# Two-layer hybrid decoder step on one core: gate's first low-rank product from mixed inputs, and three smaller moves

## Chip, core and metric

One core of one Trainium2 chip. The metric is device time of one execution in microseconds. The kernel before ran three times: 2744.53, 2752.41 and 2752.92 us, median 2752.41. A profiled execution took 2749.91 us. Engines: TensorE (PE, with its weight loads as PEld), VectorE (DVE), ScalarE (ACT), GpSimd (POOL) and SyncE (SP, which only issues transfers); ACT and POOL issue transfers too.

## Reference

One inference step of two layers for 1040 prompt tokens (16 of them meta tokens) and 8 decode tokens, width 1024, fp32. Layer 0 mixes tokens by a gated causal convolution of width 31, layer 1 by RWKV-7 with 16 heads of 64; each is followed by a squared-ReLU MLP of width 4096, and a last RMSNorm gives y. What the change touches:

```python
xx = prev - h                         # prev: the token before
xr, xw, xk, xv, xa, xg = (h + xx * x_mix[i] for i in range(6))
r, k, v = xr @ w_r, xk @ w_k, xv @ w_v
w_log = -softplus(-(w0 + tanh(xw @ w1) @ w2)) - 0.5
a = sigmoid((a0 + (xa @ a1) @ a2))
g = sigmoid(xg @ g1) @ g2             # g1: 1024 x 128
...
return out, full[:, -CONV_BUF:]       # conv state: the last 30 rows of every sequence
...
y = h * rsqrt(mean(h * h) + eps) * norm_final
```

The states (the last 30 convolution rows among them) are outputs beside y.

## The kernel before, in words

Values lie with the features on the partitions (8 tiles `k` of 128 features) and tokens along the free axis. Tokens go in groups: three for layer 0 and for the end of layer 1 (groups `g` of 352/348/348 and 328/352/352), four for the RWKV mixers (272/256/256/264, the last with the 8 decode tokens). The dense products of the MLPs and projections are split into a high and a low part and run as three matmuls each (L188 to L190: `hi*hi`, `hi*lo`, `lo*hi`). For these ACT casts a loaded weight (L158, `wo_hi`, `wi_hi`) and POOL subtracts the cast from it (L163, `wo_lo`, `wi_lo`); ACT squares and casts activations (L344, L141 `hh`), DVE makes their low part (L142 `hl`) and adds results to the residual (L355 `h`). A scheduler decides the order of the instructions on DVE, ACT, POOL and SP from priorities; on PE it is the order of the code in the long stages. Each engine works its own list strictly in order, and a transfer stands in the list of the engine that issues it.

**Layer 0, 250 to 600 us of the span.** PE runs the MLP of the first token group while DVE does the convolution of the next and PE and ACT do its decode tokens beside (`conv_dec`, L549). That loads the eight stored states in two tiles `sdec` of 120 rows x 1024, transposes them (L559, `pw`), copies them to `win` (L561), and per round `m` of 8 stores 29 rows x 1024 of them to the conv output (L564, `o_conv_sample`), on SP's list, with the MLP's weights around them.

**Preparation, up to 250 us.** Of the low-rank weights w1, a1 (64 columns each, side by side) and g1 (128 columns), ACT multiplies a copy with `x_mix` (L732), POOL subtracts it from the weights, and both, "own" and "prev", go to a scratch tensor `d_lr` in DRAM. With them `x_mix` needs no mixing of tokens: h times own plus the token before times prev.

**Mixers, 1080 to 1850 us.** For each group `prepare` (L858) gives hx (the group with one token ahead) and xx (DVE and POOL), and `mix(i, k)` (L877 to L880) makes one tile of mixed input on DVE, into a pool of 24 tiles: mix(0) for r, mix(2) for k, mix(3) for v, eight tiles each. `mixer_in` (L941) starts with `narrow_w` (L962) for the gate (`g_raw`, four tiles of 128x512) and the decays (`wa_raw`, four more from the same pool of four buffers), mix(0), `gate` (L991), the previous group's tail, then mix(3). `narrow` (L972) runs 16 matmuls on hx, shifted by one token for "prev" (L977, L978), and 8 more of 8 columns for the decode tokens in the last group (L980). ACT takes `p_g` by tanh into `lg` (L993, L994), `p_wa` into `lwa` (L988, L989). Behind it for every head pair `p`: keys, rates, values `pv`. Finished values go out to DRAM (`d_v`, L1041, L1045 on ACT); the chunks of 64 tokens read them back in `values(c)` (L1255), four transfers into `sv` and `uv` on ACT's list (L1262), and do the recurrence. Chunk 0 has its values once group 0 is done, in group 1's time.

**End, from 2260 us.** PE runs the MLP of groups 1 and 2 of layer 1; `final(g)` (L1574) makes the last norm. Group 0 sums squares over the eight feature tiles with `mean_parts` (L217): ACT squares, POOL and DVE add into one accumulator each (L231 `acc_f`), so PE only adds 2 tiles a block of 128 tokens (`fs`, L1597). Groups 1 and 2 keep eight squares (`fq`, L1585) and leave the sum to PE: 3 blocks x 8 tiles. Then the root (L1602, `os`), transposes (L1613, `pf`), scaling on DVE and ACT (L1616, L1618, `ot`, a half each) and two stores per block of half the width (L1620, L1622).

Of the kernel before, what the change touches and what calls it, by code (L numbers as in the profile page):

```python
# [16 lines left out]
P = 128  # L17
# [31 lines left out]
def hybrid_step(tc, x_prompt, x_sample, state_conv, state_shift, state_wkv, meta_tokens,  # L49
# [10 lines left out]
    with ctx:  # L60
# [25 lines left out]
        d_dec = dram.tile([6, DEC, D], F32, name="d_dec")  # L86
        d_lr = dram.tile([2, P, KT, 2, P], F32, name="d_lr")

# [29 lines left out]
        def vec(name, i):  # L118
            c = col[name] + i
            return pvec[:, c:c + 1]  # L120
# [269 lines left out]
        with ExitStack() as l0:  # L390
# [158 lines left out]
            def conv_dec(c, c_col):  # L549
# [5 lines left out]
                for m in range(KT):  # L555
# [7 lines left out]
                    nc.vector.tensor_mul(win, win, wdw[:, m:m + 1, :].broadcast_to([P, DEC, CW]))  # L563
                    nc.sync.dma_start(o_conv_sample[0, m, 0:CB - 1, :], sd[m // 4][m % 4 * CB + 1:(m % 4 + 1) * CB])  # L564
                    rd = decp.tile([P, DEC], F32, name=f"rd{m}", tag="rd")
# [119 lines left out]
            with ExitStack() as s:  # L685
# [38 lines left out]

                for i, parts in enumerate((((1, rwkv_w1[0]), (4, rwkv_a1[0])), ((5, rwkv_g1[0]),))):
                    own, prev = (xin.tile([P, D], F32, name=f"lr{i}{s_}", tag="xt").rearrange("p (k c) -> p k c", k=KT) for s_ in "op")
                    w = P // len(parts)
                    for q, (j, src) in enumerate(parts):
                        cs = slice(q * w, (q + 1) * w)
                        nc.sync.dma_start(own[:, :, cs], src.rearrange("(k p) c -> p k c", p=P))  # L730
                        for k in range(KT):
                            nc.scalar.activation(prev[:, k, cs], own[:, k, cs], AF.Copy, scale=vec("x_mix", j * KT + k))  # L732
                    for k in range(0, KT, 2):
                        nc.gpsimd.tensor_sub(own[:, k:k + 2], own[:, k:k + 2], prev[:, k:k + 2])
                    for s_, t in enumerate((own, prev)):
                        nc.sync.dma_start(d_lr[i, :, :, s_], t)
            hidp = pool(l0, "hidp0", 2)
# [203 lines left out]
        def mixer_in(g, tick):  # L941
# [19 lines left out]

            def narrow_w(i, name):  # L962

                out = []
                for q in range(HK):
                    raw = wide.tile([P, 4 * P], F32, name=nm(name, q) + "_raw", tag="wide")
                    v = raw.rearrange("p (a b) -> p a b", a=4)
                    nc.sync.dma_start(v, d_lr[i, :, 2 * q:2 * q + 2].rearrange("p k s c -> p (k s) c"))
                    out.append(v)
                return out  # L970

            def narrow(ws, name):  # L972
# [8 lines left out]
                return ps  # L981


            lg = lorap.tile([P, N1], F32, name=nm("lg"), tag="lg")
# [6 lines left out]
            def gate(ws):  # L991
                ps = narrow(ws, "g")
                nc.scalar.activation(lg[:, :n], ps, AF.Tanh, scale=0.5)  # L993
                nc.scalar.activation(lg[:, :n], lg[:, :n], AF.Copy, scale=0.5, bias=0.5)  # L994
# [260 lines left out]
        def values(c):  # L1255

            if c < NCH and c <= st["inv"] and c not in landed:
                landed.add(c)
                src = d_v[c * HS:(c + 1) * HS, :].rearrange("t (k q v) -> q t k v", q=2, v=HS)
                for t in (st["sv"], st["uv"]):  # L1260
                    for q in range(2):
                        nc.scalar.dma_start(t[HALF[1 - q], :, q, :], src[q])  # L1262

# [273 lines left out]
        with ExitStack() as l1:  # L1537
# [36 lines left out]
            def final(g):  # L1574
                lo, n = G2[g]
                hv = hl[g][:, :, :n]
                if g:
                    accs = [(actp, actp2)[g - 1].tile([P, cur["wide"]], F32R, name=f"fq{g}{k}", tag=f"acth{k}").bitcast(F32)
                            for k in range(KT)]
                else:  # L1580
                    accs = mean_parts(hv, n, f"f{g}", True, "facc")
                    yield 3
                for k in range(KT):
                    if g:
                        nc.scalar.activation(accs[k][:, :n], hv[:, k, :], AF.Square)  # L1585
                    if k % 2:
# [7 lines left out]
                for j, i in enumerate(starts):  # L1594
                    w = min(P, n - i)
                    for q, acc in enumerate(accs):
                        nc.tensor.matmul(ps[:w, j:j + 1], acc[:, i:i + w], ones_d[:, 0:1], start=q == 0, stop=q == len(accs) - 1)  # L1597
                ss = stat(f"os{g}", "os", 1, 4)
# [6 lines left out]
                for j, i in enumerate(starts):  # L1605
# [4 lines left out]
                    for hf in range(2):  # L1610
# [6 lines left out]
                        else:  # L1617
                            nc.vector.tensor_scalar(ot[:w, cs], pt[:w, :], ss[:w, j:j + 1], None, op0=ALU.mult)  # L1618
                        if np_:
                            nc.sync.dma_start(o_y_prompt[0, c:c + np_, cs], ot[:np_, cs])  # L1620
                        if np_ < w:
                            nc.sync.dma_start(o_y_sample.rearrange("b t d -> (b t) d")[:, cs], ot[np_:w, cs])  # L1622
                    yield 5
# [89 lines left out]
```

## Time and profile before

| | us |
|---|---|
| median of three runs | 2752.41 |
| profiled execution | 2749.91 |
| its span | 2748.2 |
| TensorE busy | 2641.3 |
| VectorE busy | 1716.6 |
| GpSimd busy | 1443.8 |
| ScalarE busy | 1122.1 |

The span is the time from the first to the last instruction of the profiled execution; 1.7 us lie around it. Its mean granted TensorE clock was 0.982 of full speed. A row of the timeline has start and duration in us, engine (a `q` behind it means its instruction queue, for issued transfers), line, operation, out<-in, and how many instructions the row stands for; a bracket gives the idle time ahead of it and what ended that. Matmul rows of fp32 stand for two instructions each. A row of busy time by stretch has the stretch and its length, busy time of PE, PEld, DVE, ACT and POOL with their instructions, granted clock, share of the 16 DMA engines and GB/s.

### The profile page before, as it was taken

How to read it: one execution, taken by the hardware profiler on the slowest of the kernel's cores; microseconds unless marked ns; L12 is line 12 of the kernel's file. 1: busy time of each engine (PE TensorE's matmuls, PEld its weight loads, DVE VectorE, ACT ScalarE, POOL GpSimd, SP SyncE). 2: the span in 40 equal slices, each digit the busy share in tenths (PEclk: the TensorE clock that was granted, in tenths of full speed). 3: DMA queues.
4: the chain of work that ended last, by engine and by line, in shares of the span. 5: the costliest groups of instructions: out<-in, count | busy, mean ns of one | idle time of the engine just before them, and what ended most of it. 6: DMA issues, size and time to landing. Idle time of an engine off the chain costs nothing. (4 is left out here: it accounts for less than half of the span.)

```text
span 2748.2 us, 51718 instructions
## 1 busy us (share of the span) xinstructions
PE 2641.3 (96%) x19948; PEld 2480.3 (90%) x19948; DVE 1716.6 (62%) x3546; ACT 1122.1 (41%) x2095; POOL 1443.8 (53%) x2054
## 2 busy tenths in 40 slices
PE   8999799999999999999999999979999999999998
PEld 8999699999999999877787787769999899999998
DVE  6999699997445345244757457576679753344433
ACT  5546345444444333333434444444543532222222
POOL 6678578878878776022111112365678663333330
PEclk9999899999999999999999999989999999999999
DMA  6663444554447442667777787786776642222211
GB/s 183 172 187 109 130 139 122 157 172 142 138 139 208 138 139 85 199 191 194 200 188 206 190 195 174 186 219 163 193 224 182 168 131 71 69 70 70 70 47 43
DMA packets 625548, 412.30 MB, mean 150 GB/s; under 512 B 121679, under 2 KB 567311, under 8 KB 625301
## 3 DMA queue, kind: packets, MB, share of 16 engines
q1 hardware_dynamic: 544643, 359.55, 46.7%
q10 hardware_dynamic: 72130, 23.61, 4.1%
q0 software_dynamic: 8528, 25.83, 2.9%
q8 instruction: 157, 2.57, 0.4%
q14 instruction: 90, 0.74, 0.1%
HBM read 344.81 MB, written 64.07 MB: 149 GB/s over the span
## 5 line engine op out<-in xcount | busy, mean ns | idle before, releaser
L163 POOL TENSOR_TENSOR wo_lo<-wo_raw,wo_hi 128x256 fp32r<-128x256 f32 x736 | 544.1, 772 | 318.7 <-ACT wo_hi L158 315.7
L163 POOL TENSOR_TENSOR wi_lo<-wi_raw,wi_hi 128x256 fp32r<-128x256 f32 x640 | 472.2, 770 | 264.8 <-ACT wi_hi L158 257.3
L188 PE MATMUL out<-hh,wo_hi 128*128 128x352 f32 (+2 forms) x1536 | 502.1, 327 | 20.3 <-DVE hl L142 13.3
L190 PE MATMUL ps_in<-m_l,wi_hi 128*128 128x352 f32 (+2 forms) x1536 | 494.2, 322 | 4.9 <-DVE m_l L286 4.8
L188 PE MATMUL ps_in<-m_h,wi_hi 128*128 128x352 f32 (+2 forms) x1536 | 495.4, 323 | 0.6 <-ACT m_h L285 0.6
L189 PE MATMUL out<-hh,wo_lo 128*128 128x352 f32 (+2 forms) x1536 | 495.6, 323 | 0.0
L190 PE MATMUL out<-hl,wo_hi 128*128 128x352 f32 (+2 forms) x1536 | 494.6, 323 | 0.0
L189 PE MATMUL ps_in<-m_h,wi_lo 128*128 128x352 f32 (+2 forms) x1536 | 491.9, 320 | 0.0
L355 DVE TENSOR_TENSOR h<-h,out 128x352 f32<-128x352 f32 (+2 forms) x768 | 385.7, 511 | 163.9 <-PE out L190 161.8
L536 DVE SCALAR_TENSOR_TENSOR cv<-u,wdw,cv 128x348 f32<-128x348 f32 (+2 forms) x720 | 377.9, 574 | 0.7
L158 ACT CAST wo_hi<-wo_raw 128x1024 fp32r<-128x1024 f32 x184 | 192.8, 1048 | 342.8 <-PE out L190 165.8
L158 ACT CAST wi_hi<-wi_raw 128x1024 fp32r<-128x1024 f32 x160 | 167.7, 1048 | 396.4 <-PE out L190 197.5
L188 PEld LDWEIGHTS out<-hh,wo_hi 128*128 128x128 f32 x1536 | 292.5, 190 | 27.3 <-DVE hl L142 15.4
L190 PEld LDWEIGHTS ps_in<-m_l,wi_hi 128*128 128x128 f32 x1536 | 288.8, 188 | 9.1 <-DVE m_l L286 8.6
L189 PEld LDWEIGHTS out<-hh,wo_lo 128*128 128x128 f32 x1536 | 291.7, 190 | 0.8
L188 PEld LDWEIGHTS ps_in<-m_h,wi_hi 128*128 128x128 f32 x1536 | 289.8, 189 | 2.6 <-ACT m_h L285 1.1
L190 PEld LDWEIGHTS out<-hl,wo_hi 128*128 128x128 f32 x1536 | 290.8, 189 | 0.2 <-DVE hl L142 0.2
L189 PEld LDWEIGHTS ps_in<-m_h,wi_lo 128*128 128x128 f32 x1536 | 289.2, 188 | 0.7
L343 DVE SCALAR_TENSOR_TENSOR ps_in<-ps_in,rs_m 128x352 f32<-128x352 f32 (+2 forms) x192 | 100.5, 524 | 247.6 <-PE ps_in L190 247.2
L142 DVE TENSOR_TENSOR hl<-ps_in,hh 128x352 fp32r<-128x352 f32 (+2 forms) x192 | 98.7, 515 | 139.7 <-ACT hh L141 139.6
L906 PE MATMUL pv<-mx,wv_raw 128*128 128x256 f32 (+2 forms) x512 | 133.1, 406 | 6.7 <-ACT rk L1082 4.7
L344 ACT ACTIVATE ps_in<-ps_in 128x352 f32<-128x352 f32 (+2 forms) x192 | 85.1, 444 | 132.1 <-DVE ps_in L343 131.7
(363 smaller groups left out, 4701.5 us busy)
## 6 DMA issues: line engine op xcount, KB each, us to landing
wi_raw<-in_w_mlp_in_dram SPq DMA_DIRECT2D x160, 512.0 KB
wo_raw<-in_w_mlp_out_dram SPq DMA_DIRECT2D x160, 512.0 KB
wk_raw<-in_rwkv_w_k_dram SPq DMA_DIRECT2D x32, 512.0 KB
wr_raw<-in_rwkv_w_r_dram SPq DMA_DIRECT2D x32, 512.0 KB
wv_raw<-in_rwkv_w_v_dram SPq DMA_DIRECT2D x32, 512.0 KB
d_ab<-ab POOLq DMA_DIRECT2D x32, 512.0 KB, 4.9
pg_raw<-in_conv_w_pw_dram SPq DMA_DIRECT2D x24, 512.0 KB
pa_raw<-in_conv_w_pw_dram SPq DMA_DIRECT2D x24, 512.0 KB
```

The lines of the kernel that those rows point to most:

```text
L142: eng_lo.tensor_sub(lo, src, hi.bitcast(F32))
L158: nc.scalar.copy(hi[:, :a * b], raw[:, :a * b])
L163: eng_lo.tensor_sub(lo[:, cs], raw[:, cs], hi[:, cs].bitcast(F32))
L188: nc.tensor.matmul(ps, w[0], act[0], start=first, stop=False)
L189: nc.tensor.matmul(ps, w[1], act[0], start=False, stop=False)
L190: nc.tensor.matmul(ps, w[0], act[1], start=False, stop=last)
L343: nc.vector.scalar_tensor_tensor(s, s, 0.0, rs()[:, :n], op0=ALU.max, op1=ALU.mult)
L344: nc.scalar.activation(s, s, AF.Square)
L355: nc.vector.tensor_add(hv[:, 4 * i + m, :], hv[:, 4 * i + m, :], ps[:, :n])
L536: nc.vector.scalar_tensor_tensor(acc[m][:, :n], ug[:, m, j:j + n], wdw[:, m, j:j + 1], acc[m][:, :n], op0=ALU.mult, op1=ALU.add)
L906: nc.tensor.matmul(ps[:, :n], w[:, k, :], act[k], start=k == 0, stop=k == KT - 1)
```

## The change

1. The gate's product reads mixed inputs. `gate` runs 8 matmuls on mix(5, k), which DVE makes (8 tiles a group), with g1 as it is, loaded in two tiles of 128x4x128. It stands ahead of mix(0). The preparation of g1 (L732) goes.
2. `values(0)` goes from ACT's list to POOL's; the other chunks stay.
3. The eight stores of 29 rows (L564) go from SP's list to ACT's.
4. `final` of groups 1 and 2 uses `mean_parts` as group 0 does, and each block of y is stored with one transfer of full width (two where prompt and decode tokens share a block).

```diff
-                    nc.sync.dma_start(o_conv_sample[0, m, 0:CB - 1, :], sd[m // 4][m % 4 * CB + 1:(m % 4 + 1) * CB])
+                    nc.scalar.dma_start(o_conv_sample[0, m, 0:CB - 1, :], sd[m // 4][m % 4 * CB + 1:(m % 4 + 1) * CB])
...
-                for i, parts in enumerate((((1, rwkv_w1[0]), (4, rwkv_a1[0])), ((5, rwkv_g1[0]),))):
...
+                for cs, j, src in ((HALF[0], 1, rwkv_w1[0]), (HALF[1], 4, rwkv_a1[0])):
...
+            gate_w = lambda: narrow_w("g", [rwkv_g1[0].rearrange("(k p) c -> p k c", p=P)[:, q * HK:(q + 1) * HK] for q in range(2)])
+            rate_w = lambda: narrow_w("wa", [d_lr[:, 2 * q:2 * q + 2].rearrange("p k s c -> p (k s) c") for q in range(HK)])
...
             def gate(ws):
-                ps = narrow(ws, "g")
+                ps = bank(nm("p", "g"))[:, :n]
+                for k in range(KT):
+                    nc.tensor.matmul(ps, ws[k // HK][:, k % HK, :], mix(5, k), start=k == 0, stop=k == KT - 1)
...
-            wg, ww = narrow_w(1, "g"), narrow_w(0, "wa")
+            wg, ww = gate_w(), rate_w()
+            gate(wg)
             act = mixed(0)
-            gate(wg)
...
-                        nc.scalar.dma_start(t[HALF[1 - q], :, q, :], src[q])
+                        (nc.scalar if c else nc.gpsimd).dma_start(t[HALF[1 - q], :, q, :], src[q])
...
-                if g:
-                    accs = [(actp, actp2)[g - 1].tile([P, cur["wide"]], F32R, name=f"fq{g}{k}", tag=f"acth{k}").bitcast(F32)
-                            for k in range(KT)]
-                else:
-                    accs = mean_parts(hv, n, f"f{g}", True, "facc")
-                    yield 3
+                accs = mean_parts(hv, n, f"f{g}", True, "facc")
+                yield 3
...
-                        if np_:
-                            nc.sync.dma_start(o_y_prompt[0, c:c + np_, cs], ot[:np_, cs])
-                        if np_ < w:
-                            nc.sync.dma_start(o_y_sample.rearrange("b t d -> (b t) d")[:, cs], ot[np_:w, cs])
+                    if np_:
+                        nc.sync.dma_start(o_y_prompt[0, c:c + np_, :], ot[:np_, :])
+                    if np_ < w:
+                        nc.sync.dma_start(o_y_sample.rearrange("b t d -> (b t) d"), ot[np_:w, :])
```

Lines of the changed file stand 1 to 5 off in the rows below. PE in group 1, around the gate (`mx_5_k` are the new mixtures, `hx` the unmixed input, `vt` the next work), before and then after:

```order
L921 MATMUL pn_12755<-sq_6_13612,hsel 128x256
L977 MATMUL p_g<-hx_12728,g_0_raw 128x256
L978 MATMUL p_g<-hx_12728,g_0_raw 128x256
...
L977 MATMUL p_g<-hx_12728,g_3_raw 128x256
L978 MATMUL p_g<-hx_12728,g_3_raw 128x256
L1038 MATMUL vt_7_13690<-ident,vv_7_13530 128x128 x2
```

```order
L918 MATMUL pn_12742<-sq_6_13599,hsel 128x256
L993 MATMUL p_g<-mx_5_0_13636,g_0_raw 128x256
L993 MATMUL p_g<-mx_5_1_13639,g_0_raw 128x256
...
L993 MATMUL p_g<-mx_5_7_13657,g_1_raw 128x256
L1039 MATMUL vt_7_13681<-ident,vv_7_13517 128x128 x2
```

The gate keeps its place on PE with 8 matmuls where 16 stood.

ACT in group 1, from the gate's tanh to the decays' (`r` is the key norm's root that DVE's reciprocal waits for), before and then after:

```order
L994 ACTIVATE lg_13635<-lg_13635 128x256
L1041 DMA d_v<-vt_7_13691 128x2x128
L1045 DMA d_v<-vm_7_13697 16x128
L1262 DMA sv<-d_v 64x8x64
L936 ACT_TABLE_LOAD
L936 ACTIVATE r_13765<-r_13765 128x256
```

```order
L995 ACTIVATE lg_13622<-lg_13622 128x256
L1042 DMA d_v<-vt_7_13682 128x2x128
L1046 DMA d_v<-vm_7_13688 16x128
L933 ACT_TABLE_LOAD
L933 ACTIVATE r_13756<-r_13756 128x256
L1083 COPY rk_0_13782<-pr_0_13743 128x256
```

The reads of d_v no longer stand between its writes and the root. They stand on POOL behind `d_bv` of the last head pair and ahead of a memset of `ni` and of xx for group 2.

ACT in layer 0, around the stores of the conv rows, before and then after:

```order
L158 CAST wi_0_6_hi<-wi_0_6_raw 128x1024
L158 CAST wi_0_7_hi<-wi_0_7_raw 128x1024
L344 ACTIVATE ps_in_4_0_3297<-ps_in_4_0_3297 128x352
L141 CAST hh_4_3295<-ps_in_4_0_3297 128x352
L541 COPY u_124<-cv_3_3633 128x348
L158 CAST wo_0_2_0_hi<-wo_0_2_0_raw 128x1024
```

```order
L158 CAST wi_0_6_hi<-wi_0_6_raw 128x1024
L564 DMA out_dram<-sdec_3809 29x1024 x4
L158 CAST wi_0_7_hi<-wi_0_7_raw 128x1024
L564 DMA out_dram<-sdec_3810 29x1024
L344 ACTIVATE ps_in_4_0_3280<-ps_in_4_0_3280 128x352
L564 DMA out_dram<-sdec_3810 29x1024
L141 CAST hh_4_3278<-ps_in_4_0_3280 128x352
L564 DMA out_dram<-sdec_3810 29x1024 x2
L541 COPY u_124<-cv_3_3616 128x348
L158 CAST wo_0_2_0_hi<-wo_0_2_0_raw 128x1024
```

The eight stores stand between ACT's casts, the last two right ahead of the copy of cv and the cast of `wo_0_2_0`. On SP they stood around the load of `wi_0_9`, four ahead of it and four between it and `wo_0_3_0`; there these loads now follow each other.

More of the change, by code (lines that the diff above doesn't have):

```diff
@@ L86, in hybrid_step @@
         d_dec = dram.tile([6, DEC, D], F32, name="d_dec")
-        d_lr = dram.tile([2, P, KT, 2, P], F32, name="d_lr")
+        d_lr = dram.tile([P, KT, 2, P], F32, name="d_lr")
         vecs = [
@@ L723, in hybrid_step @@
                 nc.scalar.dma_start(d_v[META:HS, KT * HS:], zt[:HS - META].rearrange("p k t -> p (k t)"))
-                for i, parts in enumerate((((1, rwkv_w1[0]), (4, rwkv_a1[0])), ((5, rwkv_g1[0]),))):
[L726 to L736, printed above, removed]
+                own, prev = (xin.tile([P, D], F32, name=f"lr{s_}", tag="xt").rearrange("p (k c) -> p k c", k=KT) for s_ in "op")
+                for cs, j, src in ((HALF[0], 1, rwkv_w1[0]), (HALF[1], 4, rwkv_a1[0])):
+                    nc.sync.dma_start(own[:, :, cs], src.rearrange("(k p) c -> p k c", p=P))
+                    for k in range(KT):
+                        nc.scalar.activation(prev[:, k, cs], own[:, k, cs], AF.Copy, scale=vec("x_mix", j * KT + k))
+                for k in range(0, KT, 2):
+                    nc.gpsimd.tensor_sub(own[:, k:k + 2], own[:, k:k + 2], prev[:, k:k + 2])
+                for s_, t in enumerate((own, prev)):
+                    nc.sync.dma_start(d_lr[:, :, s_], t)
             hidp = pool(l0, "hidp0", 2)
@@ L960, in mixer_in, with narrow_w @@
             HK = KT // 2
-            def narrow_w(i, name):
+            def narrow_w(name, srcs):
                 out = []
-                for q in range(HK):
+                for q, src in enumerate(srcs):
                     raw = wide.tile([P, 4 * P], F32, name=nm(name, q) + "_raw", tag="wide")
                     v = raw.rearrange("p (a b) -> p a b", a=4)
-                    nc.sync.dma_start(v, d_lr[i, :, 2 * q:2 * q + 2].rearrange("p k s c -> p (k s) c"))
+                    nc.sync.dma_start(v, src)
                     out.append(v)
@@ L1596, in final @@
                     for q, acc in enumerate(accs):
-                        nc.tensor.matmul(ps[:w, j:j + 1], acc[:, i:i + w], ones_d[:, 0:1], start=q == 0, stop=q == len(accs) - 1)
+                        nc.tensor.matmul(ps[:w, j:j + 1], acc[:, i:i + w], ones_d[:, 0:1], start=q == 0, stop=q == 1)
                 ss = stat(f"os{g}", "os", 1, 4)
```

3 lines of the change are left out of this document (1 added, 2 removed).

## The prediction

> **What bounds the kernel now.** I read the page's busy times first, then busy time by stage, and last the rows around each edited line. The span and the engines' shares, from the page:
>
> ```profile
> span 2748.2 us, 51718 instructions
> PE 2641.3 (96%) x19948; PEld 2480.3 (90%) x19948; DVE 1716.6 (62%) x3546; ACT 1122.1 (41%) x2095; POOL 1443.8 (53%) x2054
> ```
>
> TensorE is busy 96% of the span, so a PE instruction taken away is worth its time unless something else is late at that place, and the other gains are PE's waits. By stage (length, then busy time of PE, PEld, DVE, ACT, POOL, then granted clock):
>
> ```profile
> 250.00:600.00 350.00, 328.56 (x2023) 322.79 (x2023) 319.06 (x645) 158.91 (x253) 268.39 (x369) 0.97 0.46 137
> 1140.00:1300.00 160.00, 152.18 (x957) 122.26 (x955) 58.43 (x145) 55.12 (x154) 33.24 (x62) 1.00 0.66 188
> 1640.00:1850.00 210.00, 188.90 (x2399) 157.52 (x2398) 146.51 (x325) 90.99 (x225) 82.91 (x140) 0.93 0.79 194
> 2260.00:2700.00 440.00, 440.00 (x2747) 439.96 (x2746) 180.30 (x346) 107.86 (x170) 158.67 (x224) 1.00 0.22 64
> 2700.00:2748.20 48.20, 39.84 (x289) 39.16 (x287) 17.52 (x39) 17.83 (x38) 0.00 (x0) 0.89 0.17 61
> ```
>
> Three stages are touched. At 250–600 PE idles 21.4 us and DVE is nearly as full (319 of 350). The mixers (1080–1850) leave PE 5 to 21 us idle a window while DVE has room. From 2260 PE never waits, until the last 48 us.
>
> **Gate, removed matmuls.** The groups of the gate's matmuls and of VectorE's mixtures (ns least/median/most), then, from PE's timeline, each token group's first gate row and the row that follows its last (start, duration):
>
> ```profile
> L977 PE MATMUL p_g<-hx,g_raw x64: 377/382/469, 1143.6 to 1634.3; 128*128 128x256 f32 x32, 128*128 128x272 f32 x16, 128*128 128x264 f32 x16
> L880 DVE SCALAR_TENSOR_TENSOR mx<-xx,pvec,hx x96: 460/484/1281, 1086.7 to 1613.7; 128x256 f32<-128x256 f32 x48, 128x272 f32<-128x272 f32 x24, 128x264 f32<-128x264 f32 x24
> ...
> 1143.61 0.62 PE L977 MATMUL p_g<-hx,g_raw 128*128 128x272 f32 x2
> 1150.95 1.31 PE L906 MATMUL pr<-mx,wr_raw 128*128 128x272 f32 x5
> 1275.91 0.59 PE L977 MATMUL p_g<-hx,g_raw 128*128 128x256 f32 x2
> 1282.82 0.49 PE L1038 MATMUL vt<-ident,vv 128*128 128x128 f32 x3
> 1441.68 0.59 PE L977 MATMUL p_g<-hx,g_raw 128*128 128x256 f32 x2
> 1448.59 0.38 PE L1038 MATMUL vt<-ident,vv 128*128 128x128 f32 x2
> 1626.38 0.61 PE L977 MATMUL p_g<-hx,g_raw 128*128 128x264 f32 x2
> 1635.10 0.42 PE L1038 MATMUL vt<-ident,vv 128*128 128x128 f32 x2
> ```
>
> The gate takes 7.34, 6.91, 6.91 and 8.72 us. Half of the matmuls go, and in the last group the eight 8-column ones as well, where 8 of 0.44 us (3.5) stay: 3.67 + 3.45 + 3.45 + 5.2 = 15.8 us. Nothing is waited for at these places now.
>
> The price is 8 more mixtures a group: 32 at 0.484 us, 15.5 us of DVE. They go into slots that DVE had earlier, and chunk by chunk mix(0) takes mix(3)'s old place and mix(3) a new one, after the previous group's last key matmul; in group 1 that is near 1276, and pv, its reader, ran at 1302.7. DVE idles over 60% of 1140–1300 and 30% of 1640–1850, which covers it. If nothing covered it, 8 × 0.484 = 3.9 us would be lost in each group (15.5 in all); I take 3 us, one group's share nearly, for the first group and for places where DVE's in-order queue is then late for something smaller.
>
> **Values(0) off ScalarE, group 1.** ACT's queue, DVE behind it, and PE behind both (the bracket: idle before, and what ended it):
>
> ```profile
> 1294.84 0.60 ACTq L1262 DMA_DIRECT2D sv<-d_v  x1
> 1295.47 1.28 ACT L936 ACT_TABLE_LOAD   x1 [11.29 <-DMA d_v<-vm]
> 1297.21 1.75 DVE L937 RECIPROCAL r<-r 128x256 f32<-128x256 f32 x1 [10.64 <-ACT r L936]
> ...
> 1285.95 2.32 PE L906 MATMUL pr<-mx,wr_raw 128*128 128x256 f32 x10
> 1293.58 0.70 PE L977 MATMUL p_wa<-hx,wa_raw 128*128 128x256 f32 x2 [1.64 <-DMA wa_raw<-d_lr]
> 1301.14 0.79 PE L1096 MATMUL l_w<-lwa,wa 64*128 64x256 f32 x1 [3.41 <-ACT lwa L988]
> 1302.68 5.82 PE L906 MATMUL pv<-mx,wv_raw 128*128 128x256 f32 x16
> ```
>
> ACT stood until the writes of d_v had landed, because the read of d_v was next in its queue; lwa came late and PE waited 3.41 us. With the read on POOL, ACT goes on at 1288; what stays is p_wa's own tanh (about 0.5 us): 2.9 saved. The 1.64 us on wa_raw go too, since two of its four loads no longer wait for buffers 2 and 3 of the gate's weights. And pv's 16 instructions took 5.82 us where 10 of pr took 2.32 (0.216 apart, so 3.6 for 16): 2.2 us, the slow stretch after the wait. Together 6.8. What POOL now holds back is its next rows, a memset and xx of the next group. By their order they are needed some tens of us later, so I cost them at nothing; without that cover it would be the same wait, about 7 us, moved.
>
> On that slow pv the Trainium skill, TensorE: Matmul & The Clock Gate, Part 1, says an array that has idled runs at half rate until some microseconds of work have passed. The rows agree here (0.36 us apart against 0.216); by it, a wait that moves elsewhere would take its slow matmuls along.
>
> **Group 2.** ScalarE's order puts lg ahead of the norm's table loads. The waiting row:
>
> ```profile
> 1453.89 2.93 PE L906 MATMUL pr<-mx,wr_raw 128*128 128x256 f32 x6 [2.26 <-ACT lg L993]
> ```
>
> The bank's reader was late by 2.26 us, and 6 instructions at 0.216 need 1.46 with their tail, not 2.93: 3.7 us. Mixers: 15.8 + 6.8 + 3.7 − 3 = **23.3 us**, bounds 11 (all new mixtures paid) and 26.5.
>
> **Conv rows (SP to ScalarE).** A 4 us stretch (last two columns: share of the 16 DMA engines, GB/s), the page's group of POOL's subtractions (busy us, mean ns), then rows of SP's queue, PE and ACT by time:
>
> ```profile
> 298.00:302.00 4.00, 3.46 (x23) 3.17 (x22) 4.00 (x10) 1.88 (x4) 3.04 (x5) 1.00 0.07 27
> L163 POOL TENSOR_TENSOR wo_lo<-wo_raw,wo_hi 128x256 fp32r<-128x256 f32 x736 | 544.1, 772 | 318.7 <-ACT wo_hi L158 315.7
> ...
> 292.93 3.28 SPq L564 DMA_DIRECT2D out_dram<-sdec  x3
> 301.13 0.41 PE L188 MATMUL out<-hh,wo_hi 128*128 128x352 f32 x1
> 301.35 14.54 SPq L564 DMA_DIRECT2D out_dram<-sdec  x4
> 318.75 0.43 PE L188 MATMUL out<-hh,wo_hi 128*128 128x352 f32 x1 [2.61 <-DVE hl L142]
> 335.49 1.04 ACT L158 CAST wo_hi<-wo_raw 128x1024 fp32r<-128x1024 f32 x1 [17.35 <-DMA wo_raw<-in_w_mlp_out_dram]
> 337.88 0.66 PE L559 MATMUL pw<-ident,sdec 120*128 120x120 f32 x2 [14.85 <-ACT win L561]
> ```
>
> A share of 0.07 is one of 16 engines: each 29-row store (118.8 thousand bytes) takes 4.4 us on it at 27 GB/s, all eight 35 us, and the weights queued between and behind them wait with them. SP stands 14.54 us to issue the last four, the weights behind them land at 335.5, and PE loses 14.85 + 2.61 and two gaps of under 1 us, 18.9 in all. (PE's releaser is put down to win; the cast of wo_raw came just before, so it is the weights.)
>
> After, the weights are on SP ahead of or without the rows, and ScalarE is the one that stands. On SP the three rows from 292.93 on took 3.28 us, the last of them until 296.2, when some three quarters of the first were through; so about three and a quarter fit outstanding. The eighth then issues when 4.75 are done: 293 + 4.75 × 4.4 = 314, less if more fit, more for weights that now share the engine: 310 to 318. Behind the eighth in ScalarE's queue are the copy of cv and the cast of wo_0_2_0, which ran at 296.7. Copy and cast take 1.5 us, and PE needs about three of POOL's subtractions (0.77 us each) after them, so it can go on some 3.7 us after the eighth issue, t. PE then starts at t + 3.7 what it ran at 301.1: a stall of 12.6 (t = 310) to 20.6 (t = 318). Against the 18.9 that go this is a gain of 6 to a loss of 2; at t = 314 **2 us are gained**, which I take. Bounds: 18.9 gained if ScalarE is never held (nearest row: x3 in 3.28 us), and 17 lost if it is held to the end of all eight, near 333 (nearest row: x4 in 14.54 us).
>
> The Trainium skill, DMA: Bandwidth & Descriptors, section Issuing engines are not separate DMA queues, says that transfers run on the same 16 engines whoever starts them. By that the rows keep their 35 us on one engine after the move, as my term has it, and no more than the issue order is won. No run here has yet shown two queues sharing that one engine.
>
> **Tail.** The small products of the last norm, the longest run of them, the accumulating adds as group 0 has them, and the last store's issue:
>
> ```profile
> L1597 PE MATMUL fs<-ones_d,fq x96: 164/250/250, 2709.9 to 2739.4; 128*128 128x1 f32 x64, 128*96 128x1 f32 x32
> 2736.33 3.28 PE fs L1597 x34
> L231 DVE TENSOR_TENSOR acc_f<-acc_f,sq_f x3: 486/1035/1039, 2155.3 to 2158.9; 128x328 f32<-128x328 f32 x3
> 2744.83 0.32 SPq L1622 DMA_DIRECT2D out_dram<-ot  x1
> ```
>
> 34 instructions in 3.28 us are 0.0965 us each; 36 go in each of groups 1 and 2. In group 1 that is 36 × 0.0965 = 3.5 us on an engine that never waits there: 3.3 taken, since 12 must now follow the adds. In group 2 the last 3.28 become about 1.0, but three DVE adds (0.5 to 1.04 each) come after the last squares, and the eight transposes in between hide about half: 1.7 gained. Four wide stores for eight halves: the last issue at 2744.83 comes about 2 us sooner, of which the transfers, already under way, give 1. Also 0.5 of interleaved products. **6.5 us**, bounds 3 (adds all exposed) and 9.
>
> **Rest.** The preparation loses eight scalings, subtractions and three DMAs in a stage where PE is full: nothing, from −1 to +1.
>
> **Sum.** 23.3 + 2 + 6.5 = 31.8 us off the profiled execution's 2749.91 (span 2748.2 plus 1.7 around it): 2718.1. The runs' median is 2752.41, 2.5 higher; I forecast **2718.5**.
>
> **Rivals.**
> (a) *The rows disappear from PE's path.* ScalarE is held briefly and the weights, on their own queue, are early: 17 us better, **2701**. For it: the two queues separate weights from rows. Against: SP's 14.54 us; the number of rows that wait in a queue should be the same.
> (b) *ScalarE is held until nearly all rows are out* (t near 331): 331 + 3.7 − 301.1 = 33.6 us of stall, 14.7 worse than before: **2735**. For it: weights on the same engine; against: the fourth row was issued within 4 us.
> (c) *The gate's gain is eaten by DVE:* only 11 of 23 in the mixers: **2730**. For it: VectorE is the busiest after PE in 1640–1850; against: its share of 70%.
> (d) *Wait moved, not removed:* POOL's queue now holds xx and d_p, group 1 keeps its 6.8: **2725**.
> (e) *Slower than before:* the place is 250–600, where ScalarE feeds conv and MLP in order. If the one engine gives the weights' packets two thirds of its turns, a row takes 13.2 us and the eighth issues 4.75 × 13.2 = 63 us after 293: t = 356, a stall of 58.6, 39.7 worse than before, against 29.8 gained elsewhere: **2760**. From t = 346 on the kernel is slower than before. Against: once the weights lie ready their turns end, and their buffers come free only as PE goes on.
>
> **How the numbers follow.** Forecast (conv within 6 gained and 4 lost, mixers 19–26) 0.56, its range 2712–2726; (a) 0.14; (b) 0.10; (c) 0.08; (d) 0.06; (e) 0.06. A measurement tells about 0.3% (8.3 us) from no change, so faster means below 2744: the forecast, (a) and (d), and (b) and (c) but for the case that both hold: 0.90; within 0.3% 0.06 (that case, and half of (e)); slower 0.04. The range goes from (a) with all bounds good, 2698, to (b) with (c), 2745.
>
> **What would show it.** p_g of each group is 3.5 us long and l_w waits under 1 us; in group 1 the reciprocal runs near 1287; lg of group 2 ends no PE wait. ScalarE's rows show four long issues ending at 310–318, and PE one stall there with no wait for wo_raw at 335. The last fs run has about ten instructions, and the last store is issued some 3 us after the last norm's square root, where it was 5.2 (2739.63 to 2744.83). Wrong would be: PE waiting for mx, ScalarE released before 303 or after 325, the weights still late, or POOL's xx ending a wait.

## Result and profile after

The changed kernel takes **2723.31 us**, median of four runs (2719.99 to 2725.47), against 2752.24 us of four runs before: ratio 0.9901, 95% interval 0.9887 to 0.9915. Run again beside three experiments it had 2727.33 us, ratio 0.9920 (0.9907 to 0.9934). Forecast was 2718.5, in a range of 2698 to 2745.

The profiled execution of the changed kernel took 2719.99 us, the shortest of the four. Its page begins (busy time and share of each engine, instructions):

```profile
span 2718.1 us, 51431 instructions
PE 2613.6 (96%) x19796; PEld 2456.3 (90%) x19796; DVE 1736.2 (64%) x3584; ACT 1114.4 (41%) x2083; POOL 1447.8 (53%) x2060
```

TensorE lost 27.7 us of work and the span 30.1 us; PE's share stayed at 96%. So the time came off as PE work, and nearly as much PE idle time as before is left (104.5 us of the span, 106.9 before). Where it lies is best seen by cutting every profile at the same instructions. The marks are: start of the span, first `ps_o` matmul (a product of layer 0), the cast of `wi_0_6` on ScalarE, last `ps_o` (of L188), first `p_g` of the four groups, first and last `ps_oo` (a product of layer 1; last of L188), the last norm's root (`os`), end. A column `→x` is the length in us from the mark before it to x, taken from the starts of those rows in the kernel's own trace (e1 to e12 are the experiments below; "rows" are the conv stores):

| kernel | →ps_o | →wi_0_6 | →last ps_o | →p_g0 | →p_g1 | →p_g2 | →p_g3 | →ps_oo | →last ps_oo | →os | →end |
|---|---|---|---|---|---|---|---|---|---|---|---|
| before | 228.0 | 61.0 | 561.3 | 293.3 | 132.3 | 165.8 | 184.7 | 170.7 | 423.5 | 519.0 | 8.6 |
| after | 225.8 | 58.7 | 562.3 | 293.5 | 127.4 | 162.0 | 180.8 | 167.1 | 420.8 | 510.9 | 8.8 |
| e9 after again | 227.1 | 58.7 | 563.2 | 293.0 | 126.8 | 163.9 | 179.8 | 170.2 | 421.0 | 511.0 | 8.7 |
| e1 values(0) ACT | 226.9 | 58.7 | 562.8 | 294.3 | 128.7 | 165.7 | 181.3 | 167.6 | 420.5 | 511.0 | 9.0 |
| e10 the same | 228.5 | 58.7 | 562.5 | 292.9 | 128.8 | 166.3 | 182.0 | 170.5 | 421.5 | 510.9 | 9.0 |
| e2 rows SP | 228.8 | 58.7 | 563.3 | 292.9 | 127.3 | 162.8 | 180.4 | 168.2 | 425.9 | 511.2 | 8.8 |
| e11 the same | 228.0 | 58.8 | 562.0 | 292.9 | 127.0 | 164.2 | 181.3 | 169.1 | 420.8 | 510.8 | 8.7 |
| e3 gate old | 225.6 | 59.1 | 562.2 | 292.7 | 130.6 | 164.4 | 185.6 | 171.0 | 423.0 | 510.8 | 9.4 |
| e4 rows wide | 229.2 | 58.7 | 538.8 | 295.1 | 126.9 | 162.9 | 181.7 | 167.9 | 419.3 | 510.8 | 8.7 |
| e5 rows 28+1 | 226.2 | 58.7 | 542.0 | 292.8 | 127.1 | 163.6 | 182.7 | 168.6 | 422.2 | 511.1 | 8.7 |
| e6 before, rows wide | 228.4 | 59.0 | 538.8 | 295.0 | 131.9 | 166.1 | 185.2 | 169.9 | 419.0 | 519.8 | 9.4 |
| e7 wide, xx POOL | 228.4 | 58.7 | 539.2 | 293.2 | 127.0 | 163.7 | 181.8 | 169.9 | 424.8 | 511.0 | 8.7 |
| e8 wide, y halves | 228.5 | 58.7 | 538.8 | 292.6 | 126.9 | 165.7 | 181.4 | 170.9 | 420.2 | 511.0 | 9.1 |
| e12 wide, values(0) ACT | 228.5 | 58.7 | 539.1 | 292.7 | 127.1 | 167.6 | 182.3 | 168.8 | 424.2 | 510.8 | 9.0 |

Read columns, and distrust differences of a single pair: kernels whose instructions are the same in a stretch differ there by up to 4 us in →ps_o and in the mixers' stretches and 7 in →last ps_oo, by under 0.5 us in →wi_0_6 (but for before itself) and by under 1 in →os.

**The gate.** Its matmuls and VectorE's mixtures, by line, from the changed kernel's trace (ns least/median/most, first and last start):

```profile
L993 PE MATMUL p_g<-mx,g_raw x64: 379/382/393, 1140.3 to 1613.8; 128*128 128x256 f32 x32, 128*128 128x272 f32 x16, 128*128 128x264 f32 x16
...
L877 DVE SCALAR_TENSOR_TENSOR mx<-xx,pvec,hx x128: 460/485/1287, 1083.1 to 1612.2; 128x256 f32<-128x256 f32 x64, 128x272 f32<-128x272 f32 x32, 128x264 f32<-128x264 f32 x32
```

The PE work is what was forecast: 64 instructions for 144. A mixture still takes 0.485 us in the median.

**Group 1**, in order of time, from the timelines of PE, DVE, ACT, POOL and SP of the changed kernel:

```profile
1275.36 1.28 ACT L933 ACT_TABLE_LOAD   x1 [2.89 <-DMA xa<-d_ab]
1277.10 1.75 DVE L934 RECIPROCAL r<-r 128x256 f32<-128x256 f32 x1 [2.24 <-ACT r L933]
1281.23 1.40 POOL L1263 DMA_DIRECT2D sv<-d_v  x2 [6.75 <-issue]
1283.93 0.70 PE L1097 MATMUL l_w<-lwa,wa 64*128 64x256 f32 x2
1283.99 0.55 SPq L866 DMA_DIRECT2D hx<-d_hn  x1
1284.95 3.72 PE L903 MATMUL pv<-mx,wv_raw 128*128 128x256 f32 x16
1296.29 1.17 DVE L870 TENSOR_TENSOR xx<-hx 128x256 f32<-128x256 f32 x2 [2.93 <-DMA hx<-d_hn]
1299.95 0.46 DVE L1110 SCALAR_TENSOR_TENSOR rk<-st,negs,pb 128x256 f32<-128x256 f32 x1
1300.47 1.22 PE L1097 MATMUL l_a<-lwa,wa 64*128 64x256 f32 x2 [6.05 <-DVE rk L1110]
1301.62 4.05 PE L903 MATMUL pv<-mx,wv_raw 128*128 128x256 f32 x12
```

Up to pv everything came as forecast: ScalarE goes on at 1275, the reciprocal follows, no wait at l_w, pv at full speed (3.72 us for 16), 17.3 us after the gate's start where it was 26.8. Then 6.05 us are given back one head pair later. PE's l_a waits for a bank (an accumulator) that VectorE's `rk` (L1110) has to read; in VectorE's list that stands behind xx of group 2, and xx waits for hx, whose load was issued only when p_wa, the last reader of the old hx, had run, and took 12 us to land. In the kernel before, VectorE stood at the same load, but PE came later and had no wait at l_a there:

```profile
1309.14 0.42 DVE L873 TENSOR_TENSOR xx<-hx 128x256 f32<-128x256 f32 x1 [2.96 <-DMA hx<-d_hn]
```

**Groups 2 and 3**, timelines of PE and ACT:

```profile
1448.63 0.63 ACT L1487 ACTIVATE eq<-ey 128x512 f32<-128x512 f32 x1 [2.84 <-DVE ey L1486]
1450.09 0.30 ACT L1490 ACTIVATE ems<-ems,eps_t 128x8 f32<-128x8 f32 x1 [0.83 <-DVE ems L1489]
1450.41 1.28 ACT L987 ACT_TABLE_LOAD   x1
1451.70 0.38 ACT L987 ACTIVATE lwa<-p_wa 64x256 f32<-64x256 f32 x1
1452.13 0.79 PE L1097 MATMUL l_w<-lwa,wa 64*128 64x256 f32 x1 [4.76 <-ACT lwa L987]
1453.67 4.82 PE L903 MATMUL pv<-mx,wv_raw 128*128 128x256 f32 x12
...
1618.63 1.60 PE L903 MATMUL pr<-mx,wr_raw 128*128 128x264 f32 x6 [1.54 <-ACT lg L994]
1621.57 0.66 PE L1463 MATMUL yn<-ident,ey 128*128 128x128 f32 x4 [1.33 <-ACT gg L1288]
```

In group 2 the 2.26 us at lg are gone, and the same ScalarE chain (output norm of earlier tokens, second piece: ey, eq, ems, a table load) now stands ahead of lwa: 4.76 us, and the 12 matmuls of pv after it take 4.82 us, where 16 took 3.72 in group 1. In group 3, lg is late by 1.54 us where nothing was waited for before, and gg behind it.

**Conv rows**, the timelines of ACT and PE:

```profile
288.79 5.15 ACTq L564 DMA_DIRECT2D out_dram<-sdec  x4
294.13 9.25 ACTq L564 DMA_DIRECT2D out_dram<-sdec  x2
303.43 0.45 ACT L141 CAST hh<-ps_in 128x352 fp32r<-128x352 f32 x1 [7.97 <-issue]
303.45 10.88 ACTq L564 DMA_DIRECT2D out_dram<-sdec  x2
304.49 0.66 PE L188 MATMUL out<-hh,wo_hi 128*128 128x352 f32 x1 [9.59 <-DVE hl L142]
314.37 0.45 ACT L541 COPY u<-cv 128x348 f32<-128x348 f32 x1 [10.49 <-issue]
317.81 0.66 PE L188 MATMUL out<-hh,wo_hi 128*128 128x352 f32 x1 [10.79 <-DVE h L355]
```

And busy time in two 4 us stretches of it (length; PE, PEld, DVE, ACT, POOL with instructions; granted clock; DMA share; GB/s):

```profile
298.00:302.00 4.00, 0.00 (x0) 0.00 (x0) 0.00 (x0) 0.00 (x0) 0.00 (x0) 0.50 0.06 25
310.00:314.00 4.00, 0.00 (x0) 0.00 (x0) 0.00 (x0) 0.00 (x0) 0.00 (x0) 0.50 0.07 27
```

ScalarE was released at 314.3 and PE went on 3.5 us later. The hold comes in two pieces, because hh between the stores is held as well: 9.59 + 10.79 = 20.4 us. In the two stretches shown the DMA share is that of one engine of 16, at 25 to 27 GB/s, and all four compute engines stand.

**End**, the last norm's sums by line:

```profile
L1592 PE MATMUL fs<-ones_d,acc_f x36: 166/250/271, 2231.5 to 2709.1; 128*128 128x1 f32 x24, 128*96 128x1 f32 x8, 128*72 128x1 f32 x4
```

The same matmuls in the last group, the root and the stores, in the timelines of PE, ACT and SP:

```profile
2697.92 14.75 SPq L1615 DMA_DIRECT2D out_dram<-ot  x6
2708.12 1.17 PE L1592 MATMUL fs<-ones_d,acc_f 128*128 128x1 f32 x10
2709.32 0.41 ACT L1597 ACTIVATE os<-fs,eps_t 128x2 f32<-128x2 f32 x2 [1.20 <-PE fs L1592]
2712.72 1.05 SPq L1617 DMA_DIRECT2D out_dram<-ot  x1
```

From the root to the end it is 8.8 us, as before, though the last store is issued 3.4 us after the root and not 5.2.

### The profile page after: what moved, and what is told of

The parts are those of the page before. It is cut to its first block, busy times and chain, and to the rows that moved or that the text cites. A ratio compares the mean times of both kernels' runs of the same rounds, so it can differ in the third digit from the quotient of the medians.

```text
span 2718.1 us, 51431 instructions
## 1 busy us (share of the span) xinstructions
PE 2613.6 (96%) x19796; PEld 2456.3 (90%) x19796; DVE 1736.2 (64%) x3584; ACT 1114.4 (41%) x2083; POOL 1447.8 (53%) x2060
## 5 line engine op out<-in xcount | busy, mean ns | idle before, releaser
L188 PE MATMUL out<-hh,wo_hi 128*128 128x352 f32 (+2 forms) x1536 | 502.3, 327 | 36.4 <-DVE hl L142 18.8
L188 PE MATMUL ps_in<-m_h,wi_hi 128*128 128x352 f32 (+2 forms) x1536 | 495.3, 322 | 1.2 <-ACT m_h L285 1.2
L355 DVE TENSOR_TENSOR h<-h,out 128x352 f32<-128x352 f32 (+2 forms) x768 | 385.8, 511 | 166.6 <-PE out L190 164.4
L188 PEld LDWEIGHTS out<-hh,wo_hi 128*128 128x128 f32 x1536 | 292.8, 191 | 42.9 <-DVE hl L142 20.8
L158 ACT CAST wo_hi<-wo_raw 128x1024 fp32r<-128x1024 f32 x184 | 192.9, 1048 | 328.2 <-PE out L190 166.5
L188 PEld LDWEIGHTS ps_in<-m_h,wi_hi 128*128 128x128 f32 x1536 | 290.1, 189 | 3.1 <-ACT m_h L285 1.8
L142 DVE TENSOR_TENSOR hl<-ps_in,hh 128x352 fp32r<-128x352 f32 (+2 forms) x192 | 98.6, 515 | 132.2 <-ACT hh L141 132.1
```

The lines of the kernel that those rows point to most:

```text
L142: eng_lo.tensor_sub(lo, src, hi.bitcast(F32))
L158: nc.scalar.copy(hi[:, :a * b], raw[:, :a * b])
L188: nc.tensor.matmul(ps, w[0], act[0], start=first, stop=False)
L355: nc.vector.tensor_add(hv[:, 4 * i + m, :], hv[:, 4 * i + m, :], ps[:, :n])
```

## Experiments

Runs e1 to e4, e5 to e8 and e9 to e12 each stand beside runs of the kernel before on the same chip; a ratio is to those. Of the theories set against each other, A says for the mixers that a wait that goes is followed by the next one, and for the conv rows that their shape, not the queue, is the cost.

**e1 and e10: values(0) back on ScalarE.**

```diff
-                        (nc.scalar if c else nc.gpsimd).dma_start(t[HALF[1 - q], :, q, :], src[q])
+                        nc.scalar.dma_start(t[HALF[1 - q], :, q, :], src[q])
```

> The changed kernel (2723.3 us) with values(0) back on ScalarE's list. Theory A: in group 1 the next limit, right behind the wait that the move took away, is the load of hx for group 2 (landed at 1296.3, VectorE's xx and the rk of L1110 behind it, PE's l_a waited 6.05 us), so undoing the move costs little: the wait at l_w comes back (2 to 4 us), l_a's wait shrinks by about as much, p_g of group 2 stays within 2 us of 1429.7; 2721 to 2726. Rival B: the move earned what the prediction had for it, 5 to 7 us that l_a's wait does not eat; then 2728 to 2731.

Measured 2728.35 us (2726.54 to 2737.71), ratio 0.9929 (0.9915 to 0.9943). By the time, B. But the 2723.3 us that it is held against come from another group of runs, so both kernels were run side by side:

> The changed kernel itself, beside the next three on the same chip, since stages with the same instructions have differed by up to 4 us between the profiles so far. Both theories: ratio to before 0.989 to 0.991, and a length of the stretch from group 1's first p_g to group 2's anywhere between 162 and 166 us.

> values(0) back on ScalarE's list, beside the changed kernel. Theory A (the load of hx ends group 1's waits in either order, l_a starts 32.5 to 33.5 us after p_g): within 3 us of the changed kernel's median of this call. Rival B (the move is worth 5 us or more, as the first run of this kernel had it): 5 us or more above it.

e9 has 2727.33 us (ratio 0.9920, just above the 0.989 to 0.991 expected; group 1's stretch 163.9, as expected), e10 2732.02 (2723.97 to 2733.31), ratio 0.9931 (0.9919 to 0.9944): 4.7 us above, between the two theories. PE's waits in group 1 of e10:

```profile
1290.73 0.70 PE L1097 MATMUL l_w<-lwa,wa 64*128 64x256 f32 x2 [2.38 <-ACT lwa L987]
1304.32 1.22 PE L1097 MATMUL l_a<-lwa,wa 64*128 64x256 f32 x2 [4.11 <-DVE rk L1110]
1359.71 1.13 PE L1229 MATMUL A<-xa,bk 64*128 64x128 f32 x14 [1.56 <-DVE nr L1239]
```

The first two rows are as theory A has them: the wait at l_w is back with 2.38 us, and l_a's has shrunk from 6.59 (e9) to 4.11; l_a starts 32.9 us after the gate (1271.4) here and 34.1 in e9. The theory missed what comes after: 3 to 4 us are lost in the recurrence and the second pair behind it. The third row, the matmul of tile `A` that waits for nr, is part of that and not in e9; what makes up the rest is not shown.

**e12: the same on the wide-copy kernel.**

> The wide-copy kernel (2701.7) with values(0) back on ScalarE's list: the same question without the hold of the conv rows ahead of it. Theory A: ratio to before within 0.001 of the wide copy's 0.9832. Rival B: 0.985 or above.

2708.78 us, ratio 0.9851 (0.9836 to 0.9866), against 0.9832 without it: B by a hair, with the wide copy's ratio from another group of runs.

**e3: the gate as before** (16 matmuls on hx, g1 prepared, behind mix(0); the other three parts as changed).

```diff
-                ps = bank(nm("p", "g"))[:, :n]
-                for k in range(KT):
-                    nc.tensor.matmul(ps, ws[k // HK][:, k % HK, :], mix(5, k), start=k == 0, stop=k == KT - 1)
+                ps = narrow(ws, "g")
...
```

> The changed kernel with the gate, its weights and their preparation as before (16 matmuls on hx, g1 prepared). Theory A: a shorter gate shows fully as time on PE in each group but is partly eaten by the next wait, so the old gate costs 11 to 16 us in the mixers, plus 2 us in the preparation stage if the scalings of g1 held that up: 2735 to 2742, with p_g of each group 6.9 to 8.7 us long. Rival B: the mixers lose the full 15.8 us and the waits in group 1 and 2 do not come back elsewhere: 2742 or above. Rival C: the preparation costs nothing and its 2 us in the changed kernel were a chance of the start: then ScalarE's cast of wi_0_6 stands within 1 us of the changed kernel's 284.5, else near 287 to 289.

2738.58 us (2736.07 to 2744.50), ratio 0.9964 (0.9950 to 0.9977): A for the time. For the preparation it is C: the cast of wi_0_6 stands at 284.7, the preparation costs 59.1 − 58.7 = 0.4 us in →wi_0_6, and the 2 us at the start belong to no part, since →ps_o runs from 225.6 to 229.2 over all kernels.

e3, e1, e10 and e12 make a table of two parts in the mixers (first p_g to first ps_oo, means of the kernels' sums in us): neither 653.3 (before, e6); values(0) moved alone 651.6 (e3); gate alone 645.6 (e1, e10, e12); both 640.7 (the changed kernel, e2, e4, e5, e8, e9, e11). So what a part is worth depends on the other: values(0) is worth 1.7 us alone and 4.9 on top of the gate, the gate 7.7 alone and 10.9 on top of values(0). These are means of few profiles (e3 is a single one, the sums with both parts run from 637.3 to 644.9), so the steps hold to some 3 us. In group 1's stretch alone: 166.0, 164.4, 166.5, 163.6. There the two parts together bring 2.4 us, less than the 3.45 of the gate's matmuls, and the gate alone brings nothing.

**e2 and e11: the conv rows back on SP.**

```diff
-                    nc.scalar.dma_start(o_conv_sample[0, m, 0:CB - 1, :], ...)
+                    nc.sync.dma_start(o_conv_sample[0, m, 0:CB - 1, :], ...)
```

> The changed kernel with the eight 29-row stores back on SP's list. Theory A: the stores last 35 us on one DMA engine either way, ScalarE's hold (PE waits of 9.59 and 10.79 us) costs what SP's hold of the weights did (18.9 in all) or 1 to 2 us more: 2721 to 2724, with PE waiting for weights near 330 and not for hl and h. Rival B: the move earned 2 us or more, as the prediction took it: 2725 or above.

2729.15 us (2725.68 to 2730.72), ratio 0.9922 (0.9911 to 0.9934): B by the time, but the stretch that holds the rows is 563.3 us against 562.3, and most of the rest lies at the start and in →last ps_oo, where the instructions are the same. So it was run again beside the changed kernel:

> The eight stores back on SP's list, beside the changed kernel. Theory A (the hold only changes its place): within 3 us of the changed kernel's median of this call. Rival B (the move is worth 5 us or more, as the first run had it): 5 us or more above it.

2726.30 us (2721.72 to 2731.07) against 2727.33: A. The stretch is 562.0 us against 563.2. With the stores on SP the hold is there too, at SP's issues and in PE's wait for the weights behind them (e2):

```profile
301.69 14.54 SPq L564 DMA_DIRECT2D out_dram<-sdec  x4
337.75 0.66 PE L559 MATMUL pw<-ident,sdec 120*128 120x120 f32 x2 [15.73 <-ACT win L561]
```

**e5: each store cut into 28 rows and 1 row**, on ScalarE's list at the same places.

```diff
-                    nc.scalar.dma_start(o_conv_sample[0, m, 0:CB - 1, :], ...)
+                    for r0, r1 in ((0, CB - 2), (CB - 2, CB - 1)):
+                        nc.scalar.dma_start(o_conv_sample[0, m, r0:r1, :], sd[m // 4][m % 4 * CB + 1 + r0:m % 4 * CB + 1 + r1])
```

> The changed kernel with each 29-row store cut in two, 28 rows and 1 row, on ScalarE's list at the same places. Theory A: what held ScalarE was the shape, since 29 rows of a store all went to one DMA engine; 28 rows spread over 14, so the two PE waits of 9.59 and 10.79 us go as they did with the wide copy: ratio to before 0.982 to 0.985, cast of wi_0_6 to the last ps_o 538 to 543 us. Rival B: what held it is the number of stores, or a source on few partitions, however it is cut: 560 us or more in that stretch, ratio 0.990 or above. In between (545 to 558) if the 16 issues themselves (0.3 to 0.6 us each) delay the casts.

2704.57 us (2701.11 to 2706.18), ratio 0.9833 (0.9819 to 0.9847), stretch 542.0: A. The first issues on ScalarE, and PE's waits where it had stood 9.59 and 10.79 us:

```profile
289.23 1.48 ACTq L565 DMA_DIRECT2D out_dram<-sdec  x4
290.84 0.67 ACTq L565 DMA_DIRECT2D out_dram<-sdec  x2
...
295.94 0.43 PE L188 MATMUL out<-hh,wo_hi 128*128 128x352 f32 x1 [0.43 <-DVE hl L142]
299.19 0.43 PE L188 MATMUL out<-hh,wo_hi 128*128 128x352 f32 x1 [2.03 <-DVE h L355]
```

Twice as many transfers with the same bytes, and an issue costs some 0.37 us, where pairs of the 29-row stores took 9.25 and 10.88: the shape was the cost.

**e4: one copy of all eight rows' blocks from the stored state to the output**, in DRAM, with 16 as the slowest dimension.

```diff
-                    nc.scalar.dma_start(o_conv_sample[0, m, 0:CB - 1, :], ...)
...
+                rows = lambda t: t.rearrange("m w d -> m (w d)").rearrange("m (a x) -> a m x", a=16)
+                nc.scalar.dma_start(rows(o_conv_sample[0, :, 0:CB - 1, :]), rows(state_conv[0, :, 1:CB, :]))
```

> The changed kernel with the eight stores replaced by one copy of the same rows from the stored state to the output in DRAM, cut so that the slowest dimension is 16 (16 x 8 x 1856 elements), issued once by ScalarE. Theory A: the stores held one of 16 engines for 35 us because 29 rows do not divide, and the hold was PE's only reason to wait there: the waits of 9.59 and 10.79 us go, 2703 to 2707. Rival B: VectorE's convolution (316 us busy of 350 in that stage) is the next limit and gives less than half: 2712 to 2719. Rival C: the copy's own traffic delays the weights: a new PE wait for weights of over 3 us near 290.

**2701.69 us** (2701.19 to 2707.78), ratio 0.9832 (0.9819 to 0.9845): A, 1.3 us below its range, and the best kernel of the study. The copy waits for nothing, so it is issued at 0.8 us of the span. Its stage, from busy time by stretch:

```profile
250.00:600.00 350.00, 347.49 (x2167) 343.18 (x2166) 339.54 (x690) 168.26 (x267) 285.61 (x393) 1.00 0.52 152
```

PE is busy 347.5 of 350 us (327.2 in the changed kernel), and B is out: VectorE at 339.5 keeps up. The stretch loses 23.8 us against the mean of 562.6 of the five runs with the stores on ScalarE (after, e1, e3, e9, e10): the 20.4 us of waits, and some 3 us because from 297.0 to 321.1 the granted clock was 0.50 and PE worked 5.8 us in that stretch of the changed kernel. e4 differs in place and source as well as in shape; e5 is the run that changes the shape alone.

**e6: the kernel before with only that copy.**

> The kernel before with only the eight stores replaced by the one wide copy on ScalarE's list. Theory A: the hold was worth the same there, and is independent of the rest: cast of wi_0_6 to the last ps_o falls from 561.3 to 538 to 541 us, ratio 0.991 to 0.993. Rival B: before, SP's hold cost only the 18.9 us of PE's waits and the clock after them nothing: 543 us or more, ratio 0.993 or above.

2725.12 us (2724.24 to 2728.66), ratio 0.9915 (0.9902 to 0.9928), stretch 538.8: A. This part alone is worth about what the whole change is.

**e7: the wide-copy kernel with group 2's xx all on GpSimd.**

```diff
-                (nc.gpsimd if k % 3 == 2 else nc.vector).tensor_sub(xx[:, k, :npr], ...)
+                (nc.gpsimd if g == 2 or k % 3 == 2 else nc.vector).tensor_sub(xx[:, k, :npr], ...)
```

> The wide-copy kernel with all eight xx of group 2 on GpSimd, so that VectorE's list has one mixture and no xx between the wait for hx and L1110's rk in group 1. Theory A: PE's l_a waits there for VectorE standing at the load of hx: its wait falls from 6.1 to about 4 us, first p_g of group 1 to that of group 2 from 162.9 to about 161. Rival B: the wait belongs to the mixtures or to values(0) on GpSimd, and eight subtractions (6 us) on GpSimd delay d_p and d_ab: 163 or more. Whole time within 0.2% of the wide-copy kernel's 2701.7 either way.

PE's wait in group 1 of the wide-copy kernel (e4), then DVE and PE of e7:

```profile
1282.06 1.22 PE L1098 MATMUL l_a<-lwa,wa 64*128 64x256 f32 x2 [6.14 <-DVE rk L1111]
```

```profile
1276.69 0.82 DVE L878 SCALAR_TENSOR_TENSOR mx<-xx,pvec,hx 128x256 f32<-128x256 f32 x1 [3.24 <-POOL xx L871]
1277.43 0.47 DVE L1111 SCALAR_TENSOR_TENSOR rk<-st,negs,pb 128x256 f32<-128x256 f32 x1
1277.96 1.22 PE L1098 MATMUL l_a<-lwa,wa 64*128 64x256 f32 x2 [4.14 <-DVE rk L1111]
```

The wait fell from 6.14 to 4.14 us, as A said: hx and what is ahead of rk on VectorE set it. But the stretch is 163.7 against 162.9 and the time 2705.81 (2702.04 to 2708.13), ratio 0.9838 (0.9824 to 0.9852): the 2 us are not seen at the end. A is right on the wait; the stretch is in B's range, though differences of 4 us stand there between equal kernels, so what the wait is worth stays open. A second hx tile, with which the load need not wait for p_wa, was not tried.

**e8: the wide-copy kernel with y in halves.**

```diff
-                    if np_:
-                        nc.sync.dma_start(o_y_prompt[0, c:c + np_, :], ot[:np_, :])
+                        if np_:
+                            nc.sync.dma_start(o_y_prompt[0, c:c + np_, cs], ot[:np_, cs])
...
```

> The wide-copy kernel with y stored in halves as before (sums as changed). Theory A: the full-width stores earned nothing, since the last transfers end the kernel: from the last norm's root to the end 8.6 us against 8.7 to 8.8. Rival B: they earned 1 us, as the prediction took it: 9.7 us. Whole time within 0.1% of 2701.7.

2703.22 us (2702.65 to 2705.69), ratio 0.9833 (0.9819 to 0.9847); root to end 9.1 against 8.7. Between A and B, nearer to A: wide stores earn at most some 0.4 us, and kernels that all have them differ by as much (8.7 to 9.4).

## Why the prediction came out, by its steps

- **Gate and mixers, forecast 23.3, measured 12.6** (653.3 to 640.7). The PE work was right to 0.1 us a group, and no PE wait for a mixture shows. But the 12.6 are less than the 15.8 us of PE work that went: on balance the waits earned nothing. The steps that failed are "values(0) off ScalarE, group 1" (6.8) and "group 2" (3.7): both waits went as said, and both were replaced. Group 1 kept 2.4 us of 10.3 (166.0 to 163.6), as hx's load is next, and group 2 kept 3.8 of 7.2 (185.2 to 181.4, means over all), as the norm's second piece is next; for group 2 no run tests that. Group 3 kept 1.5 of 5.2 (170.5 to 169.0), with the new waits for lg and gg. Only group 0 gave more than was said, 5.0 for 3.7 (132.1 to 127.1). The text asked "what is late next" only of POOL's queue. It called POOL's xx "needed some tens of us later", but VectorE read it some 5 us later, and VectorE's own pieces of xx, which stand ahead of rk, were not looked at. That is close to rival (d), at another engine. The parts were also added up as if each were worth the same without the other, which the comparison under e3 does not bear out.
- **Conv rows, forecast +2, measured −0.4 ± 1** (562.6 for ScalarE, 562.2 for SP: 561.3, 563.3, 562.0). The mechanism held, ScalarE standing and PE behind it, and the release came at 314.3 where 314 was worked out. The size was off because hh between the stores stalled as well, which made two waits, 20.4 us together, and not one of 16.6. Rival (a), rows off PE's path, needed another shape, not another queue (e4, e5).
- **Tail, forecast 6.5, measured 8.5**: →os fell by 8.5 (519.4 to 510.9) and →end by nothing sure. Group 2 gave what was said: end of the last out matmul to root 6.55 us before (2733.08 to 2739.63), 4.75 after (2704.57 to 2709.32). The stores' 1 us was not there (e8). So the rest, 3.8 in the forecast, gave 6.7. Part of what was missed lies behind the small products of group 1, in busy time by stretch, of before and then of after:

```profile
2717.00:2720.00 3.00, 3.00 (x33) 3.00 (x32) 0.00 (x0) 0.00 (x0) 0.00 (x0) 1.00 0.00 0
2720.00:2724.00 4.00, 4.00 (x20) 3.93 (x20) 1.99 (x5) 1.62 (x5) 0.00 (x0) 0.57 0.02 4
```

```profile
2697.00:2701.00 4.00, 4.00 (x30) 3.98 (x29) 3.25 (x8) 2.55 (x6) 0.36 (x1) 1.00 0.32 131
```

  In the first row of before three microseconds of one-column matmuls, with PE busy throughout, were followed by 4 us at a granted clock of 0.57: 4 × 0.43 = 1.7 us, which the changed kernel does not lose. That is not the whole cause. e6 has the tail of before, and there the same run of products is followed by full clock; it loses 1.54 us to a wait for `ot` and some 0.6 us in group 2's last products (4.00 us for the 34 that took 3.43 before) in its place, and its →os is no shorter (519.8):

```profile
2689.49 3.42 PE L1598 MATMUL fs<-ones_d,fq 128*128 128x1 f32 x34
2692.00:2696.00 4.00, 4.00 (x35) 3.96 (x35) 2.08 (x5) 1.90 (x5) 0.00 (x0) 1.00 0.01 3
2700.97 0.64 PE L1614 MATMUL pf<-ident,h 128*96 128x128 f32 x4 [1.54 <-DVE ot L1619]
2709.03 4.00 PE L1598 MATMUL fs<-ones_d,fq 128*128 128x1 f32 x34
```

  Why the clock fell in the one and not in the other is not shown.
- **Preparation, forecast 0**: 0.4 (e3).
- **Sum.** 12.6 − 0.4 + 8.5 + 0.4 = 21.1 us by stretches, against 22 and 29 by the two comparisons of times. Forecast 31.8. That the total came near is in good part luck. The mixers alone were taken too high by 11 us, the tail too low by 2, and the first comparison is the larger one: there before lies 2.6 us higher (2752.24 against 2749.61 beside e9) and the changed kernel 4.0 lower (2723.31 against 2727.33). Against 2727.33 the forecast of 2718.5 is 9 us too low, still within its range.

## What to carry to other kernels

Before a wait is counted as gained, read the next ten microseconds of every in-order list that took part in it: the saving lasts only until the next load or chain that was late anyway (here hx in group 1, the norm's second piece in group 2). What two changes are worth that share such a list should not be added without a run of each alone. Here the stall of stores that occupied one DMA engine was cured by their shape; moving them to another issuer moved the stall to that issuer's list. And cut several profiles at the same instructions before a difference of 3 us in 2700 is believed.

## What the runs showed of the hardware

- A store of 29 rows from 29 partitions ran on one engine of 16 (share 0.06 to 0.07 at 25 to 27 GB/s; by that some 4.4 us a store, an estimate); 28 rows and one row instead let the whole stretch run 20 us sooner (562.6 to 542.0). The Trainium skill, DMA: Bandwidth & Descriptors, section Why a DMA increments its semaphore by 16 and not by 1, says that the number of engines is the largest up to 16 that divides the slowest dimension of both sides. The runs agree on 29 rows; that 28 and 16 spread is seen only in the waits that went (PE's 9.59 and 10.79 us to 0.43 and 2.03 in e5).
- An engine that issues can stand at it, with all its compute behind: ScalarE's issues took 9.25 and 10.88 us for two stores each, and its cast and copy behind them waited 7.97 and 10.49; SP's took 14.54 us for four.
- The granted TensorE clock can fall where PE is shown busy: to 0.57 over the 4 us behind 34 instructions of one column (before). It need not: in e6 it stayed at 1.00 behind the same instructions.
- Stretches with the same instructions differed between executions by up to 4 us at the start and in the mixers and up to 7 between first and last `ps_oo`, and by under 1 us in →os. What makes the difference is not shown.
